# One block of a diffusion transformer on one core: an adaLN part moved in front of the MLP's normalization, VectorE's order there fixed, and the last rows of the first up products taken in two halves

## The chip, the core and the metric

The kernel runs on one core of one Trainium2 chip. What is measured is the time of one execution on the device in microseconds (us). A core has TensorE for products (PE in the profile, with its weight loads as PEld), VectorE (DVE), ScalarE (ACT), GpSimd (POOL), and SyncE (SP), whose queue issues nearly all loads here. All engines run side by side and wait for one another through semaphores. TensorE writes into eight PSUM banks.

## What is computed

One layer works on 256 latent tokens and 256 context tokens of width 2048, all in float32. Cut to what the change touches:

```python
sh_a, sc_a, g_a, sh_m, sc_m, g_m = split(silu(c) @ w_ada + b_ada)      # adaLN: 2048 x 12288
...                                                                     # attention and pooling mixer
x  = x + g_a * (concat(attn, pool) @ w_out)                             # 2048 x 2048
hm = rms_norm(x, norm_mlp_w) * (1 + sc_m) + sh_m
x  = x + g_m * (square(relu(hm @ w_up)) @ w_down)                       # 2048 x 8192 and back
return rms_norm(x, final_norm_w)
```

## The kernel before

**Products.** Each float32 weight block (512 rows by 512 columns, 1 MB) comes into a `raw` buffer, of which there are five, and is split into a high and a low part of a shorter format: ScalarE makes `hi` (line 97), VectorE `lo` (line 98), for 256 rows at a time, which is called a half. There are six `hi` and six `lo` buffers. The activations are split in the same way, and `mm3` makes each product of three: high by high, low by high, high by low (lines 288 to 290).

**The stream of loads.** `WeightStream` holds one list of all blocks in the order in which they are used. `next` issues loads up to five blocks ahead of the block that is handed out and splits up to six halves ahead. A load can start only when its `raw` buffer is free: the buffer of a weight block is free after both splits, that of an adaLN block after the engine that works on it has read it.

**adaLN parts.** The modulation of the MLP (`m0` to `m7`, 256 of its columns of scale and of shift each) and the attention gate (`g0` to `g3`) are computed in the gaps of later stages, in four blocks of 1 MB each, as `ADA_LATE` and the `LATE_...` numbers say. Parts marked "pe" are 32 small products per part (line 305, moving 128x512) and one copy `ada_e` (line 311); parts marked "dve" are sixteen VectorE instructions `ada_v` (lines 325 and 327) per part. `finish` then turns the row into columns with eight small products (`ps_adac`, line 335) and adds it into `am` and `sm` (lines 340 to 344). The finish of a part is called at the beginning of the step after its fourth.

**Around the change.** The output projection has four column groups (`out_group`), each of four weight blocks; beside them run `m2` to `m4` on VectorE. After a group VectorE multiplies by the gate and adds (lines 853 and 854), ScalarE sums squares (line 855), and TensorE transposes the new `x` into `x2T` (line 834). After the last group follows a chain: the sum of squares, its inverse root on VectorE (lines 862 to 866), a product that spreads it over partitions (`ps_r`, line 868), the copy `rb` (line 870), and then `modulate_m`, which makes four rows of `hm` of 128 channels each: `x2T` times `am` and `rb` (line 882), ScalarE's high part (line 884) and VectorE's low part (line 885). `first_up_groups` then works on three column groups of the up projection together, four rows after four rows (`kg`), with 48 products of 128x256 per block. `m5` runs on TensorE before its first products, `m6` and `m7` on VectorE beside them; the last rows (12 to 15) need `m6` and `m7`. Then come `down_group` and `up_group` in turn up to the end.

**What sets the order.** The program is traced in the order of the code; a scheduler then orders each engine's instructions by a timeline that it simulates, and keeps that order at run time: each engine takes its list in sequence. `tc.issue_after(ins)` forces what a block issues on the engine of `ins` behind `ins`. Some of the lines in question:

```python
LATE_OUT = (0, 1, 1, 1) * 4
LATE_NORM = 4
LATE_UP = (1,) * 8 + (0,) * 4
```

Of the kernel before, what the change touches and what calls it, by code (L numbers as in the profile page):

```python
# [15 lines left out]
P = 128  # L16
D = 2048
KC = 16
# [20 lines left out]
LATE_OUT = (0, 1, 1, 1) * 4  # L39
LATE_NORM = 4  # L40
LATE_UP = (1,) * 8 + (0,) * 4
# [17 lines left out]
class WeightStream:  # L59
# [7 lines left out]
    def __init__(self, nc, pool):  # L67
        self.nc, self.pool = nc, pool
        self.items, self.raw, self.split = [], {}, {}
        self.halves, self.n_load, self.n_half, self.n_used, self.pos = [], 0, 0, 0, 0  # L70
        self.hold, self.last = True, ()
# [16 lines left out]
    def split_to(self, n):  # L88
        nc = self.nc
        while self.n_half < min(n, len(self.halves)) and not self.hold:  # L90
# [8 lines left out]
            self.last = (up.ins, low.ins)  # L99
            self.split[i, h] = (hi, lo)  # L100
# [24 lines left out]
def kernel(  # L125
# [117 lines left out]

    for i in range(12):
        add_up(i % 3, i // 3)
        for _ in range(LATE_UP[i] + (LATE_NORM if i == 0 else 0)):
            add_in(("late",))
# [266 lines left out]
    def late_steps():  # L514
        for what, j, engine in ADA_LATE:
            ada, weights, spread = (ada_pe, sel, selb) if engine == "pe" else (ada_dve, ones[:, 0:2], ones)

            def finish(e, what=what, j=j, weights=weights, spread=spread):
                if what == "m":
                    k = slice(2 * j, 2 * j + 2)  # L520
                    ps = ada_cols(e, weights)
                    ada_scale(am[:, k], ps[:, 0:2], bcol[:, 64 + 2 * j : 66 + 2 * j], cols[:, 48 + 2 * j : 50 + 2 * j])
                    ada_shift(sm[:, k], ps[:, 2:4], bcol[:, 48 + 2 * j : 50 + 2 * j])
# [7 lines left out]
            yield from steps[:4]  # L531
            late_finish.append(steps[4])

    late_finish = []
    late_iter = late_steps()

    def run_late(n):

        for _ in range(n):
            f = next(late_iter, None)  # L540
            while late_finish:
                late_finish.pop()()
            if f:
                f()
# [292 lines left out]
    def out_group(dg):  # L837
# [11 lines left out]
        ds_ = slice(512 * dg, 512 * dg + 512)  # L849
        for i in range(2):  # L850
            t = wop.tile([P, 512], F32, tag="t", name="t", bufs=3)
            xs = x2[:, i, ds_]
            nc.vector.tensor_tensor(t, pss[i], gate["a"][:, ds_], ALU.mult)
            nc.vector.tensor_tensor(xs, xs, t, ALU.add)
            nc.scalar.activation(t, xs, AF.Square, accum_out=ss2[:, i, dg : dg + 1])

    for dg in range(4):
        out_group(dg)
    transpose_group(3)

# [16 lines left out]
    def modulate_m(kg):  # L877

        for j in range(4):
            k = 4 * kg + j  # L880
            v = x2T[kg][:, j, :]
            nc.vector.scalar_tensor_tensor(v, v, am[:, k, 0:1], rb, ALU.mult, ALU.mult)
            hi, lo, both = parts(k)
            nc.scalar.activation(hi, v, AF.Identity, bias=sm[:, k, 0:1])  # L884
            nc.vector.scalar_tensor_tensor(lo, v, sm[:, k, 0:1], hi.bitcast(F32), ALU.add, ALU.subtract)
            hm.append((hi, lo, both))
# [35 lines left out]
    def first_up_groups():  # L922
# [7 lines left out]
        modulate_m(0)  # L930
        for kg in range(4):
            for f in range(3):
                w = S.next("w")
                if kg == f == 0:
                    with tc.issue_after(rb_ready.ins):
                        run_late(LATE_NORM)
                for m in range(4):
                    for j in range(4):
                        k = 4 * kg + j
                        mm3(sums[f][m], w(j, slice(P * m, P * m + P)), hm[k], k == 0 and m % 2 == 0, k == KC - 1)  # L940
                with tc.issue_after(rb_ready.ins):
                    run_late(LATE_UP[3 * kg + f])
                    if kg == 2 and f == 1:
                        run_late(1)
                if kg < 3 and f == 1:
                    modulate_m(kg + 1)
                if kg == 3:
                    acts.append(activation(sums[f]))
# [153 lines left out]
```

## Time and profile before

| | us |
|---|---|
| median of 3 runs | 1146.16 |
| lowest and highest of them | 1143.71, 1147.84 |
| the profiled execution, whole | 1147.05 |
| span of its trace | 1145.3 |
| TensorE busy in it | 1104.6 (96%) |
| VectorE busy | 779.2 (68%) |
| ScalarE busy | 523.6 (46%) |
| GpSimd busy | 37.0 (3%) |

The trace is of one execution, with times counted from the beginning of its span. A matmul's row shows its duration from entry to result; matmuls overlap, so the distance from one start to the next tells the pace. A share of busy time is an average over stages with different limits, so it does not tell what a stage is worth.

### The profile page before, as it was taken

Reading aid. Unit: us, or ns where it says so; the run is one execution under the profiler, and the core shown is the slowest. Engines: PE = TensorE matmul, PEld = TensorE weight load, DVE = VectorE, ACT = ScalarE, POOL = GpSimd, SP = SyncE. Lnnn points to the kernel's source line nnn. Section 1 sums busy time; section 2 is a strip of 40 time slices with the busy share of each in tenths; the row PEclk is TensorE's granted clock in tenths of the full one; section 3 lists DMA queues with packets and bytes.
Section 4 is the critical chain, followed back from the end, with each engine's and each line's share of the span. In section 5 each row is a group of like instructions: output and inputs, shape, how many; then the busy total and the mean of one; then the engine's idle time right before and its main releaser. Section 6 shows DMA issues by size and latency. Waiting matters only on the chain.

```text
span 1145.3 us, 16131 instructions
## 1 busy us (share of the span) xinstructions
PE 1104.6 (96%) x6364; PEld 909.3 (79%) x6364; DVE 779.2 (68%) x1222; ACT 523.6 (46%) x796; POOL 37.0 (3%) x53
## 2 busy tenths in 40 slices
PE   4999999999999989999999999999999999999996
PEld 2767778856588869888888888888888888888885
DVE  4655567875588988696774874884664565587576
ACT  4633233499734343365343443433444443443452
POOL 1000001610000000000000000000000000000000
PEclk9999999999999989899999999999999999999998
DMA  9999898687799989977775776775566556566532
GB/s 343 359 341 336 288 325 264 210 292 259 267 369 314 325 306 332 336 246 259 262 265 184 257 269 195 253 267 192 184 192 202 194 184 185 191 192 204 184 110 75
DMA packets 174013, 286.66 MB, mean 250 GB/s; under 512 B 5608, under 2 KB 72352, under 8 KB 172784
## 3 DMA queue, kind: packets, MB, share of 16 engines
q1 hardware_dynamic: 172800, 279.55, 72.9%
q0 software_dynamic: 848, 5.55, 1.3%
q8 instruction: 50, 0.82, 0.3%
q10 hardware_dynamic: 288, 0.52, 0.1%
q14 instruction: 27, 0.22, 0.1%
HBM read 283.50 MB, written 2.10 MB: 249 GB/s over the span
## 4 chain that ended last, share of the span: by engine, by line
PE 88%; DVE 4%; ACT 3%; DMA 3%; issue 1%; SPq 0%; ACTq 0%; DVEq 0%
PE ps_up L919 25%; PE ps_d L288 10%; PE ps_d L289 10%; PE ps_d L290 10%; PE ps_ada L305 4%; PE ps_w L288 3%; PE ps_w L290 3%; PE ps_w L289 3%; PE ps_qu L288 2%; PE ps_qu L290 2%; PE ps_qu L289 2%; PE ps_up L288 1%; DVE lo L98 1%; PE ps_o L763 1%; PE ps_up L289 1%; PE ps_up L290 1%
## 5 line engine op out<-in xcount | busy, mean ns | idle before, releaser
L98 DVE TENSOR_TENSOR lo<-raw,hi 128x1024 fp32r<-128x1024 f32 x330 | 397.7, 1226 | 211.8 <-ACT hi L97 201.0
L97 ACT CAST hi<-raw 128x1024 fp32r<-128x1024 f32 x330 | 338.1, 1050 | 409.1 <-PE ps_up L919 151.7
L919 PE MATMUL ps_up<-mx,hi 128*128 128x512 f32 x832 | 200.1, 393 | 0.0
L288 PE MATMUL ps_d<-hi,ahi 128*128 128x512 f32 (+1 forms) x520 | 200.0, 386 | 0.0
L289 PE MATMUL ps_d<-lo,ahi 128*128 128x512 f32 (+1 forms) x520 | 200.0, 386 | 0.0
L290 PE MATMUL ps_d<-hi,alo 128*128 128x512 f32 (+1 forms) x520 | 198.7, 386 | 0.0
L919 PEld LDWEIGHTS ps_up<-mx,hi 128*128 128x128 f32 x832 | 153.4, 188 | 31.8 <-issue 1.9
L290 PEld LDWEIGHTS ps_d<-hi,alo 128*128 128x128 f32 x520 | 97.7, 188 | 19.8
L288 PEld LDWEIGHTS ps_d<-hi,ahi 128*128 128x128 f32 x520 | 97.7, 188 | 19.5
L289 PEld LDWEIGHTS ps_d<-lo,ahi 128*128 128x128 f32 x520 | 97.7, 188 | 19.3
L919 PEld LDWEIGHTS ps_up<-mx,lo 128*128 128x128 f32 x832 | 106.7, 191 | 4.0
L327 DVE SCALAR_TENSOR_TENSOR ada_v<-raw,c_sil,ada_v 128x512 f32<-128x512 f32 x135 | 100.9, 748 | 12.7 <-DMA raw<-in_w_ada_dram 11.1
L919 PE MATMUL ps_up<-mx,lo 128*128 128x256 f32 x832 | 107.9, 283 | 0.0
L288 PE MATMUL ps_qu<-hhi,hi 128*128 128x256 f32 x240 | 69.3, 290 | 1.4 <-ACT hi L97 1.4
L305 PE MATMUL ps_ada<-raw,c_sil 128*32 128x512 f32 x480 | 68.3, 628 | 2.2 <-DMA raw<-in_w_ada_dram 1.9
L290 PE MATMUL ps_qu<-hhi,lo 128*128 128x256 f32 x240 | 67.0, 282 | 0.3 <-DVE lo L98 0.3
L289 PE MATMUL ps_qu<-hlo,hi 128*128 128x256 f32 x240 | 66.9, 280 | 0.0
L288 PEld LDWEIGHTS ps_qu<-hhi,hi 128*128 128x128 f32 x240 | 45.1, 188 | 16.6 <-issue 8.4
L288 PE MATMUL ps_up<-mx,hi 128*128 128x256 f32 x192 | 54.7, 293 | 1.8 <-ACT mx L884 1.5
L289 PE MATMUL ps_up<-mx,hi 128*128 128x256 f32 x192 | 54.3, 287 | 0.0
L290 PE MATMUL ps_up<-mx,lo 128*128 128x256 f32 x192 | 53.1, 287 | 0.4 <-DVE lo L98 0.4
L288 PE MATMUL ps_w<-hi,mx 128*128 128x512 f32 x128 | 50.4, 395 | 0.0
(202 smaller groups left out, 1336.4 us busy)
## 6 DMA issues: line engine op xcount, KB each, us to landing
raw<-in_w_ada_dram SPq DMA_DIRECT2D x128, 512.0 KB, 7.3
raw<-in_w_mlp_up_dram SPq DMA_DIRECT2D x64, 1024.0 KB, 5.5
raw<-in_w_mlp_down_dram SPq DMA_DIRECT2D x64, 1024.0 KB, 5.1
raw<-in_w_ada_dram SPq DMA_DIRECT2D x32, 1024.0 KB, 6.8
raw<-in_w_in_dram SPq DMA_DIRECT2D x19, 1024.0 KB, 7.6
raw<-in_w_out_dram SPq DMA_DIRECT2D x16, 1024.0 KB, 7.5
xnat<-in_x_dram SPq DMA_DIRECT2D x2, 1024.0 KB, 6.0
xnat<-in_ctx_dram SPq DMA_DIRECT2D x2, 1024.0 KB, 11.7
```

Source lines behind the costliest of these rows:

```text
L97: up = nc.scalar.copy(hi, raw)
L98: low = nc.vector.tensor_tensor(lo, raw, hi.bitcast(F32), ALU.subtract)
L288: nc.tensor.matmul(ps, a[0], b[0], start=first, stop=False, skip_group_check=True)
L289: nc.tensor.matmul(ps, a[0], b[1], start=False, stop=False, skip_group_check=True)
L290: nc.tensor.matmul(ps, a[1], b[0], start=False, stop=last, skip_group_check=True)
L305: nc.tensor.matmul(ps[32 * j : 32 * j + 32, :], c_sil[:, 4 * kg + j, :], raw[:, j, :], start=(kg == 0), stop=(kg == 3), tile_position=(0, ...
L327: nc.vector.scalar_tensor_tensor(box["e"], raw[:, j, :], sc, box["e"], ALU.mult, ALU.add)
L763: nc.tensor.matmul(ps[64 * i : 64 * i + 64, 0:T], va[k // 2][:, k % 2, 64 * g : 64 * g + 64], pT[:, k, i, :], start=(k == 0), stop=(k == 3 ...
L919: nc.tensor.matmul(ps, wk, h, start=part == k == 0, stop=part == 1 and k == KC - 1, skip_group_check=True)
```

## The change

No weight block, product or VectorE operation is added or taken away; their order and places change.

- `LATE_OUT` shifts the twelve steps of `m2` to `m4`: one stands after the very first block of the output projection, and none after its last.
- The four blocks of `m5` come before the first up block in the list of loads. Their products are traced right behind the last output product (`behind_output`), ahead of VectorE's multiplication and addition and of the last transpositions. The small column products of `m4` stand behind them, those of `m5` behind the transpositions; what VectorE does with both (`rest`) is put off until after the first up block.
- The first up block (`up00` below) is no longer split ahead of time. Its first half is split behind the last addition of the output stage, its second behind the four VectorE instructions of line 882 for rows 0 to 3. Splits of later blocks come behind the low parts of rows 0 to 3.
- `modulate_m` takes a list of rows and makes all products with `am` and `rb` and the high parts first, then the low parts.
- The products with `up00` go in three passes: high by high over all rows and columns, low weights by high rows, high weights by low rows.
- Rows 12 to 15 are taken as 12 and 13 for all three column groups, then 14 and 15 for all three. Rows 14 and 15 are modulated behind `m7`'s finish. The three blocks of the last rows are all held at once, which takes all six half buffers; splits of the first down blocks are released as those halves are used up. The three `activation` calls come within the second pass.

```diff
-LATE_OUT = (0, 1, 1, 1) * 4
+LATE_OUT = (1, 1, 1, 1) + (0, 1, 1, 1) * 2 + (0, 1, 1, 0)
 LATE_NORM = 4
-LATE_UP = (1,) * 8 + (0,) * 4
+LATE_UP = (0,) + (1,) * 8 + (0,) * 3
...
+    for _ in range(LATE_NORM):
+        add_in(("late",))
     for i in range(12):
         add_up(i % 3, i // 3)
-        for _ in range(LATE_UP[i] + (LATE_NORM if i == 0 else 0)):
+        for _ in range(LATE_UP[i]):
             add_in(("late",))
...
+                    if put_off is None:
+                        rest()
+                    else:
+                        put_off.append(rest)
...
-    for dg in range(4):
+        return add.ins
+
+    for dg in range(3):
         out_group(dg)
+
+    def behind_output():
+
+        nonlocal put_off
+        before = late_finish[:]
+        late_finish.clear()
+        S.hold, put_off = True, []
+        run_late(LATE_NORM)
+        for f in before:
+            f()
+
+
+    added = out_group(3, behind_output)
+    S.hold = False
+    with tc.issue_after(added):
+        S.split_to(S.n_half + 1)
+    S.hold = True
     transpose_group(3)
+    finish_late()
+    late_rest, put_off = put_off, None
...
+    def modulate_m(ks, between=None):
+
+        new = [parts(k) for k in ks]
+        hm.extend(new)
+        for part in range(2):
+            for k, (hi, lo, _) in zip(ks, new):
+                v = x2T[k // 4][:, k % 4, :]
+                if part == 0:
+                    low = nc.vector.scalar_tensor_tensor(v, v, am[:, k, 0:1], rb, ALU.mult, ALU.mult)
+                    up = nc.scalar.activation(hi, v, AF.Identity, bias=sm[:, k, 0:1])
+                else:
+                    low = nc.vector.scalar_tensor_tensor(lo, v, sm[:, k, 0:1], hi.bitcast(F32), ALU.add, ALU.subtract)
+            if between and part == 0:
+                with tc.issue_after(low.ins):
+                    between()
+        return low.ins, up.ins
...
+        behind, up = modulate_m(range(4), second_half)
+        with tc.issue_after(behind), tc.issue_after(up):
+            w = S.next("w")
+
+            for a, h in ((0, 0), (1, 0), (0, 1)):
+                for k in range(4):
+                    for m in range(4):
+                        nc.tensor.matmul(sums[0][m], w(k, slice(P * m, P * m + P))[a], hm[k][h],
+                                         start=a == h == k == 0 and m % 2 == 0, stop=False, skip_group_check=True)
+            w = S.next("w")
+            behind = S.low[S.pos - 1, 1]
+            with tc.issue_after(behind):
+                for rest in late_rest:
+                    rest()
+                products(1, w, range(4))
+                run_late(LATE_UP[1])
+                modulate_m(range(4, 8))
+            products(2, S.next("w"), range(4))
+            run_late(LATE_UP[2])
+        for kg in (1, 2):
             for f in range(3):
...
+                products(f, S.next("w"), range(4 * kg, 4 * kg + 4))
+                run_late(LATE_UP[3 * kg + f])
+                if f == 1:
+                    modulate_m((8, 9, 10, 11) if kg == 1 else (12, 13))
+
+        used = S.n_used + N_HALF
+        ws = [S.next("w")]
+        finish_late()
+        modulate_m((14, 15))
+        S.hold = True
+        ws += [S.next("w") for _ in range(2)]
+        S.hold = False
+        for k, free in ((12, (1, 1, 1)), (14, (3, 5, 6))):
+            for f in range(3):
+                products(f, ws[f], (k, k + 1))
+                S.split_to(used + free[f])
+                if k == 14:
                     acts.append(activation(sums[f]))
         return acts
```

## Rows read from the trace of the kernel before

**Rows 1.** The page: busy time, share of the span and instructions per engine.

```profile
PE 1104.6 (96%) x6364; PEld 909.3 (79%) x6364; DVE 779.2 (68%) x1222; ACT 523.6 (46%) x796; POOL 37.0 (3%) x53
```

**Rows 2.** Stretches: busy PE, PEld, DVE, ACT, POOL; granted clock, DMA share, GB/s.

```profile
330.00:402.00 72.00, 72.00 (x340) 60.03 (x339) 62.22 (x81) 30.09 (x42) 0.00 (x0) 1.00 0.97 326
402.00:409.00 7.00, 3.01 (x20) 2.46 (x18) 5.09 (x24) 2.00 (x5) 0.55 (x1) 0.92 0.89 327
409.00:415.40 6.40, 6.40 (x33) 1.36 (x32) 6.40 (x20) 3.14 (x8) 0.00 (x0) 0.55 0.52 162
409.00:479.00 70.00, 67.15 (x529) 61.42 (x529) 60.19 (x97) 29.05 (x39) 0.00 (x0) 0.94 0.94 322
475.00:483.00 8.00, 6.05 (x31) 5.99 (x32) 5.16 (x12) 0.91 (x2) 0.00 (x0) 0.58 1.04 385
493.00:1134.00 641.00, 641.00 (x3229) 546.30 (x3229) 428.35 (x557) 279.18 (x371) 0.53 (x1) 1.00 0.63 208
```

**Rows 3.** Timeline of the first gap: start, duration, engine, line, tiles, idle before.

```profile
401.87 0.60 PE L834 MATMUL tp_x<-ident,x 128*128 128x128 f32 x4
...
404.33 0.16 DVE L862 TENSOR_REDUCE ssum<-ss 128x2 f32<-128x8 f32 x1 [0.85 <-ACT t L855]
...
408.31 3.26 DVE L882 SCALAR_TENSOR_TENSOR x2T<-x2T,am,rb 128x256 f32<-128x256 f32 x8
408.83 3.31 ACT L884 ACTIVATE mx<-x2T,sm 128x256 fp32r<-128x256 f32 x8 [4.02 <-DVE x2T L882]
...
409.00 6.49 PE L305 MATMUL ps_ada<-raw,c_sil 128*32 128x512 f32 x32
...
415.41 0.50 PE L288 MATMUL ps_up<-mx,hi 128*128 128x256 f32 x2
```

**Rows 4.** The chain that ended last: the same products where the clock is full.

```profile
242.11 3.57 PE ps_ada L305 x32
...
421.42 0.79 PE ps_adac L335 x8
```

**Rows 5.** Loads: splits that waited for one, the first gate product, issues on SP.

```profile
322.05 2.00 ACT L97 CAST hi<-raw 128x1024 fp32r<-128x1024 f32 x2 [6.07 <-DMA raw<-in_w_out_dram]
...
331.62 0.68 DVE L853 TENSOR_TENSOR t<-ps_w,ga 128x512 f32<-128x512 f32 x1
...
396.20 0.92 SPq L84 DMA_DIRECT2D raw<-in_w_ada_dram  x2
...
399.35 0.92 SPq L84 DMA_DIRECT2D raw<-in_w_ada_dram  x2
...
410.99 0.37 SPq L84 DMA_DIRECT2D raw<-in_w_mlp_up_dram  x1
```

**Rows 6.** Issue to landing (us, last number) of the loads issued at 396.20 and 399.35.

```profile
raw<-in_w_ada_dram SPq DMA_DIRECT2D x2, 512.0 KB, 7.3
...
raw<-in_w_ada_dram SPq DMA_DIRECT2D x2, 512.0 KB, 7.1
```

**Rows 7.** Timeline of VectorE: its longest wait in the first up products.

```profile
462.15 1.23 DVE L98 TENSOR_TENSOR lo<-raw,hi 128x1024 fp32r<-128x1024 f32 x1 [2.76 <-ACT hi L97]
```

**Rows 8.** Timeline of TensorE around the second gap.

```profile
475.44 1.13 PE L335 MATMUL ps_adac<-ones,ada_v 128*128 128x2 f32 x8 [0.67 <-DVE ada_v L327]
478.08 1.22 PE L288 MATMUL ps_up<-mx,hi 128*128 128x256 f32 x4 [1.51 <-ACT mx L884]
...
480.17 0.41 PE L289 MATMUL ps_up<-mx,hi 128*128 128x256 f32 x1
480.38 0.41 PE L290 MATMUL ps_up<-mx,lo 128*128 128x256 f32 x1
...
483.23 0.28 PE L288 MATMUL ps_up<-mx,hi 128*128 128x256 f32 x1
483.35 0.28 PE L289 MATMUL ps_up<-mx,hi 128*128 128x256 f32 x1
```

**Rows 9.** The first down products by tile: duration min/median/max, first and last start.

```profile
L288 PE MATMUL ps_d<-hi,ahi x520: 278/389/396, 493.3 to 1134.6; 128*128 128x512 f32 x168, 128*128 128x256 f32 x6
```

More of the change, by code (lines that the diff above doesn't have):

```diff
@@ L70, in __init__ @@
         self.halves, self.n_load, self.n_half, self.n_used, self.pos = [], 0, 0, 0, 0
-        self.hold, self.last = True, ()
+        self.hold, self.last, self.low = True, (), {}
     def add(self, kind, *loads, halves=2):
@@ L99, in split_to @@
             self.last = (up.ins, low.ins)
+            self.low[i, h] = low.ins
             self.split[i, h] = (hi, lo)
@@ L530, in late_steps, with last, finish_late @@
             steps = ada(finish)
-            yield from steps[:4]
-            late_finish.append(steps[4])
-    late_finish = []
+            yield from steps[:3]
+            def last(steps=steps):
+                steps[3]()
+                late_finish.append(steps[4])
+            yield last
+    late_finish, put_off = [], None
     late_iter = late_steps()
+    def finish_late():
+        while late_finish:
+            late_finish.pop(0)()
     def run_late(n):
@@ L835, in transpose_group, with out_group @@
             nc.scalar.copy(x2T[dg][:, :, P * i : P * i + P], tp.rearrange("p (j t) -> p j t", j=4))
-    def out_group(dg):
+    def out_group(dg, then=None):
         pss = [bank("ps_w0"), bank("ps_w1")]
@@ L849, in out_group @@
         ds_ = slice(512 * dg, 512 * dg + 512)
+        if then:
+            then()
         for i in range(2):
@@ L853, in out_group @@
             nc.vector.tensor_tensor(t, pss[i], gate["a"][:, ds_], ALU.mult)
-            nc.vector.tensor_tensor(xs, xs, t, ALU.add)
+            add = nc.vector.tensor_tensor(xs, xs, t, ALU.add)
             nc.scalar.activation(t, xs, AF.Square, accum_out=ss2[:, i, dg : dg + 1])
-    for dg in range(4):
+        return add.ins
+    for dg in range(3):
         out_group(dg)
+    def behind_output():
[11 more added lines that the diff above has]
+    S.hold = True
     transpose_group(3)
+    finish_late()
+    late_rest, put_off = put_off, None
     ssum = wop.tile([P, 2], F32, name="ssum")
@@ L875 @@
     hm = []
[L877 to L886, printed above, removed]
+    def modulate_m(ks, between=None):
[13 more added lines that the diff above has]
+        return low.ins, up.ins
     def activation(pss):
@@ L929, in first_up_groups, with products @@
         acts = []
-        modulate_m(0)
-        for kg in range(4):
-            for f in range(3):
[L933 to L947, printed above, removed]
+        def products(f, w, ks, ms=range(4)):
+            for m in ms:
+                for k in ks:
+                    mm3(sums[f][m], w(k % 4, slice(P * m, P * m + P)), hm[k], k == 0 and m % 2 == 0, k == KC - 1)
@@ new lines, in second_half @@
+        def second_half():
+            S.hold = False
+            S.split_to(S.n_half + 1)
+        behind, up = modulate_m(range(4), second_half)
[16 more added lines that the diff above has]
+            run_late(LATE_UP[2])
@@ new lines, in first_up_groups @@
+        for kg in (1, 2):
+            for f in range(3):
+                products(f, S.next("w"), range(4 * kg, 4 * kg + 4))
[4 more added lines that the diff above has]
+        ws = [S.next("w")]
+        finish_late()
+        modulate_m((14, 15))
+        S.hold = True
+        ws += [S.next("w") for _ in range(2)]
+        S.hold = False
+        for k, free in ((12, (1, 1, 1)), (14, (3, 5, 6))):
[3 more added lines that the diff above has]
+                if k == 14:
```

7 lines of the change are left out of this document (3 added, 4 removed).

## The prediction

> **What bounds the kernel now.** I read the page first: TensorE is busy 96% of the span [rows 1], so only its idle and its slow time can be won. Then I cut the span into stretches [rows 2]. From 330 to 402 TensorE is busy throughout at the full granted clock, and again from 493 to 1134 (641.00 of 641.00 us). What lies between holds two gaps. In the first, from 402 to 415.4, TensorE works 3 of 7 us and then 6.4 us at a mean clock of 0.55; in the second, from 475 to 483, it works 6 of 8 us at 0.58. The chance of the change is there and nowhere else: from 401.87, where the first transpositions follow the last output product [rows 3], to 493.3, where the down products begin [rows 9], 91.4 us. The products that must be done in that time, at the full pace: 12 blocks of 48 products, 0.12 us from start to start [rows 8], 69.1 us; `m5`, 3.57 us; columns of four parts, 0.79 us each [rows 4], 3.2 us; transpositions 1.2 us (two groups of four at 0.60 [rows 3]). That is 77.1 us without the small `ps_r`, so at most some 14 us can be won, 1.2% of the whole.
>
> The timeline of the first gap says who is late in it [rows 3]. VectorE's chain goes from the sum of squares at 404.33 to the first product with `rb` at 408.31. TensorE has nothing to do beside it but transpositions, and its clock falls. Only at 409.00 come the 32 products of `m5`, at half clock in 6.49 us, and the up products wait behind them until 415.41. In the second gap TensorE waits 0.67 us for VectorE's `m7`, computes its columns, waits 1.51 us for the rows made of it, and then runs at 0.21 us a product instead of 0.12 up to about 483.1 [rows 8].
>
> **The change, part by part.** Times are those of the profiled execution, 1147.05 us with a span of 1145.3; it lies 0.9 above the median of the three runs, 1146.16.
>
> *Steps of `m2` to `m4` one place earlier: 0.* In the first column group every output block now has a load of 1 MB in front of it. The first block of the second group landed at 322.05 and is needed at about 331.6, when the gate multiplies the first group [rows 5]; its two splits take until about 325.5. One more MB costs about 3.2 us at the 326 GB/s of this stretch [rows 2], so some 3 us of the margin stay, and TensorE's full row covers the shift. Without that cover it would cost up to 3 us; below nothing it can hardly go, since TensorE has no idle time there.
>
> *`m5` and the columns between the last output product and the MLP.* From 401.87 the 32 products end at 405.4, beside VectorE's chain. The columns of `m4` and `m5` (0.79 each), the transpositions and `ps_r` also fall under it. Their data: the last block of `m5` was issued at 396.20 and landed 7.3 us after its issue [rows 5, 6], at about 404.0; it moves one MB earlier in the list, to about 401. The products need it at 404.6, so I count no wait; with the old landing the wait is nil too.
>
> *VectorE's order.* The first half of `up00` now stands between the last addition (ended at about 403.5) and the sum of squares. Through `up00` the list holds as many MB as it did through the last block of `m5`, so I let it land at 404.0. ScalarE's half takes 1.0 (two in 2.00 [rows 5]), VectorE's 1.23 [rows 7]: the sum starts at 406.3, not 404.33, 2.0 later. If the weights are there in time, the lower bound is 0.4 (403.5 plus 1.23). The upper bound is `up00` landing like the old fifth block, issued at 399.35 and landed 7.1 after its second issue, at 407.0 [rows 5, 6]: 5.0 later. The middle value is nearest to the row of equal MB. VectorE waits with everything behind that half in hand, the whole chain and with it TensorE. The trace shows VectorE idle for 2.76 us at one half whose high part was late [rows 7]. [...]
>
> With 2.0, the first product with `rb` starts at 410.3. The first up product needs one such instruction (0.48) and one high part (0.5), so it starts at 411.3 instead of 415.41. High by high goes row by row, and VectorE makes a row every 0.41 us (8 in 3.26 [rows 3]) where TensorE takes four products, 0.48; the low weights' second half (1.2) and the low rows (four times 0.41) follow in time for passes of 1.92 us each. No wait there.
>
> *The clock.* Between 405.4 and 411.3 TensorE has some 3.5 us of small work. Before, it fell to half after such a stretch, before 409, and rose again near the end of `m5`. I count one fall: in the second gap some 24 products at 0.21 instead of 0.12 lost 2.2 us [rows 8]. Bounds: 0, and 2.9 (6.49 against 3.57 [rows 3, 4]). TensorE's own list then ends at 411.3 + 2.2 + 69.1 + 1.6 (columns of `m6` and `m7`) = 484.2.
>
> *VectorE as the next bound.* From 409 to 479, when it has made the last rows (TensorE takes the first of them at 478.08 [rows 8]), it is busy 60.2 of 70 us [rows 2]. Its work does not shrink: with 0.7 before 409 and the second half of `up00`, 1.2, it is 62.1 us from the first product with `rb`. Started at 410.3 it ends at 472.4 without idle time, and at 482.2 with the 9.8 us of before. Much of that idle time waits for loads. These stop when all five buffers are held: the first up load is issued only at 410.99, after the first products of `m5` [rows 5]; with those products at 402 it is issued about 8 us earlier. I keep 4 us of idle: 476.4. Behind it come 0.5 for the high and low part and the last 72 products (rows 14 and 15), 8.6: 485.5. That is later than TensorE's own 484.2, so VectorE ends the stage; the bounds are 484.2 and 491.3. Rows 12 and 13 come first and cover the finish of `m7`, which before stood bare.
>
> *Activations within the second pass.* From the end of the first group's sums, 5.8 before the end, to the second half of the first down group, 5.4 after it, VectorE has four low halves (4.9) and sixteen instructions of 128x256 (6.6 at 0.41), 11.5 us in 11.2. I add 0.8; bounds 0 and 2.8, the longest wait of before [rows 7]. Stage end: 486.3, against 493.3. **Gain 7.0 us.** Behind it TensorE has no idle time to swallow it [rows 2], so it lasts to the end: 1147.05 − 7.0 = 1140.05, and at the level of the median 1139.2; I say 1139.
>
> **The rivals.** *Both gaps close.* The half comes in time (0.4), the clock stays, VectorE idles 2 us. First product 409.7, TensorE's list 480.4, VectorE 408.7 + 62.1 + 2 + 9.1 = 481.9: gain 11.4, 1134.8. For it: TensorE is given work where it had none. Against: the small products have two columns each, and the clock fell beside such work in the second gap.
>
> *The half of `up00` takes the gap over.* It lands at 407.0, VectorE's start moves to 413.3; with 6 us of idle 413.3 + 62.1 + 6 + 9.1 + 0.8 = 491.3: gain 2.0, 1144.2. For it: loads stand at 0.97 of the DMA engines before 402, and five blocks lie between. Against: the equal number of MB.
>
> *The change does not do what it says.* The finish of `m7` is traced ahead of the products of rows 12 and 13. If the scheduler puts its columns amid the first pass on TensorE, TensorE waits for `m7` as before [rows 8]. With columns at 475.3 and half of the first pass behind them, 36 and 72 products, 13.0, and the clock's 2.2, the end is 490.5: gain 2.8, 1143.4. For it: the columns stood so in the trace of before. Against: in a simulated timeline that is right, the ready products go first.
>
> *Slower.* All six half buffers are held by the last rows, so down weights can be split only from 5.8 us before the end, beside three activations. It decides from the point at which VectorE brings rows 14 and 15 no earlier than it would with all its old idle time (stage end 491.3): then the first down block waits 2.8 for its low half and 2.8 for the second activation, and the clock falls once more (2.2): 499.1, 5.8 later than before, 1152. Against it: VectorE has 8 us of earlier loads.
>
> **How the numbers follow.** Forecast 0.43, both gaps close 0.20, the half takes over 0.14, not what it says 0.17, slower 0.06. A measurement of this kernel tells about 0.3% from no change, 3.4 us, so faster means under 1142.7. The forecast and the first rival lie under it, and I give a quarter of the second rival and a third of the third: 0.73 faster, 0.21 the same, 0.06 slower. The range reaches from the first rival's 1134 to 1144.7, above the second and third; it leaves out the slower case, and some of the bounds on either side.
>
> **What would show it.** In the profile after: `ps_ada` of `m5` in about 3.6 us right behind the last output product; the first up product near 411; the sum of squares near 406 with VectorE waiting in front of it for a high part; the granted clock at half for some us around 412; no wait of TensorE for `ada_v` after 465; the first down product near 486. I am wrong if TensorE waits in the output stage, if VectorE idles more than 6 us up to its last rows, if the columns of `m7` still hold TensorE, or if the down groups wait for halves.

## The result, and the profile after

The change makes the kernel slower: 1154.11 us median of 7 runs (1152.56 to 1157.12) against 1147.53 for the kernel before on the same chip (7 runs, 1143.71 to 1151.12), ratio 1.0064 with a 95% interval of 1.0049 to 1.0078. The forecast was 1139, its range 1134 to 1144.7. The profiled execution has a span of 1153.8 us, 8.5 more than before.

Three cuts show where they come from: the first instruction behind the last output product, the first up product, the first down product (starts on TensorE's timeline).

| | output stage ends | first up product | first down product | first gap | first up to first down |
|---|---|---|---|---|---|
| before | 401.87 | 415.41 | 493.30 | 13.5 | 77.9 |
| forecast | 401.87 | 411.3 | 486.3 | 9.4 | 75.0 |
| after | 407.27 | 415.73 | 502.03 | 8.5 | 86.3 |

The output stage ends 5.4 us later, the first gap is 5.1 shorter, the stretch behind it 8.4 longer: +8.7. Behind the first down product both kernels take the same time, 652.0 and 651.8 us.

The page of after: busy time, share and instructions per engine. It is nearly the row of before [rows 1] (TensorE 1.7 us more) and tells nothing of the loss.

```profile
PE 1106.3 (96%) x6364; PEld 910.2 (79%) x6364; DVE 779.8 (68%) x1222; ACT 523.6 (45%) x796; POOL 35.7 (3%) x53
```

Stretches of after (busy PE, PEld, DVE, ACT, POOL; granted clock, DMA share, GB/s): two at the start of the output stage, two of the first gap, the first up products up to the end of the first pass over the last rows, the second gap.

```profile
308.00:312.00 4.00, 3.04 (x7) 1.91 (x8) 0.95 (x2) 2.46 (x5) 0.00 (x0) 0.53 1.07 362
312.00:316.00 4.00, 4.00 (x13) 3.16 (x12) 2.75 (x3) 0.92 (x1) 0.00 (x0) 0.62 0.86 301
402.00:409.00 7.00, 7.00 (x40) 4.64 (x42) 2.97 (x5) 2.44 (x4) 0.55 (x1) 1.00 0.52 184
409.00:415.40 6.40, 5.15 (x46) 3.30 (x38) 4.69 (x23) 2.79 (x7) 0.00 (x0) 1.00 0.90 305
415.73:482.06 66.33, 63.90 (x512) 61.87 (x512) 57.76 (x88) 29.19 (x37) 0.00 (x0) 1.00 0.94 318
482.00:487.00 5.00, 0.11 (x2) 0.08 (x1) 4.77 (x6) 1.16 (x2) 0.00 (x0) 0.87 1.05 392
487.00:496.00 9.00, 6.56 (x30) 6.47 (x31) 6.53 (x14) 0.91 (x2) 0.00 (x0) 0.50 0.84 294
```

The first gap went as it should: the clock is 1.00 there, where it was 0.55 before [rows 2]. But TensorE's clock now falls near 308, where the output stage begins (0.53 from 308 to 312, 0.62 from 312 to 316), and TensorE stands still from 482 to 487 (busy for 0.11 of 5.00 us). The first place on the timelines of ScalarE and TensorE (start, duration, engine, line, tiles; in brackets the idle time before and what ended it):

```profile
305.18 1.99 ACT L97 CAST hi<-raw 128x1024 fp32r<-128x1024 f32 x2 [2.78 <-DMA raw<-in_w_out_dram]
307.34 1.08 ACT L772 COPY pT<-tp_p 128x512 f32<-128x512 f32 x2
308.96 1.11 PE L781 MATMUL ps_o<-pT,va 128*64 128x256 f32 x2 [3.66 <-ACT pT L772]
```

In ScalarE's list the high part of the second output block stands ahead of the last copies `pT` of the attention. The first step of `m2` now puts a load of 1 MB ahead of that block; it comes 2.78 us late for ScalarE, the copies wait behind it, TensorE waits 3.66 us for them, and its clock falls (0.53 from 308 to 312). The same two in the trace of before, where the block is 0.42 us late and TensorE waits 1.06:

```profile
301.49 1.99 ACT L97 CAST hi<-raw 128x1024 fp32r<-128x1024 f32 x2 [0.42 <-DMA raw<-in_w_out_dram]
306.48 0.65 PE L763 MATMUL ps_o<-pT,va 128*64 128x256 f32 x2 [1.06 <-ACT pT L754]
```

The second place on VectorE's and TensorE's timelines:

```profile
478.14 2.34 DVE L98 TENSOR_TENSOR lo<-raw,hi 128x1024 fp32r<-128x1024 f32 x2
480.41 0.74 DVE L330 SCALAR_TENSOR_TENSOR ada_v<-raw,c_sil,ada_v 128x512 f32<-128x512 f32 x1
481.20 2.36 DVE L98 TENSOR_TENSOR lo<-raw,hi 128x1024 fp32r<-128x1024 f32 x2
483.48 0.74 DVE L330 SCALAR_TENSOR_TENSOR ada_v<-raw,c_sil,ada_v 128x512 f32<-128x512 f32 x1
484.14 1.22 DVE L98 TENSOR_TENSOR lo<-raw,hi 128x1024 fp32r<-128x1024 f32 x1
485.27 1.53 DVE L330 SCALAR_TENSOR_TENSOR ada_v<-raw,c_sil,ada_v 128x512 f32<-128x512 f32 x2
486.95 1.84 PE L338 MATMUL ps_adac<-ones,ada_v 128*128 128x2 f32 x8 [4.89 <-DVE ada_v L330]
491.23 1.65 PE L291 MATMUL ps_up<-mx,hi 128*128 128x256 f32 x6 [2.44 <-ACT mx L926]
```

The 24 halves of the up blocks are split by 480.4; the three at 481.20 and 484.14 belong to down blocks, and `m7`'s last instructions stand behind them. TensorE ended its first pass at 482.06 and waits 4.89 us for `m7`, where it waited 0.67 before [rows 8]. Its columns then take 1.84 us, 2.44 us pass until the rows 14 and 15, and the second pass begins at the clock of the columns (0.50 from 487 to 496).

### The profile page after: what moved, and what is told of

It reads as the page before. It is cut to its first block, busy times and chain, and to the rows that moved or that the text cites. A ratio compares the mean times of both kernels' runs of the same rounds, so it can differ in the third digit from the quotient of the medians.

```text
span 1153.8 us, 16135 instructions
## 1 busy us (share of the span) xinstructions
PE 1106.3 (96%) x6364; PEld 910.2 (79%) x6364; DVE 779.8 (68%) x1222; ACT 523.6 (45%) x796; POOL 35.7 (3%) x53
## 4 chain that ended last, share of the span: by engine, by line
PE 83%; DMA 7%; DVE 5%; ACT 4%; issue 1%; SPq 1%; ACTq 0%; DVEq 0%
PE ps_up L965 25%; PE ps_d L292 10%; PE ps_d L293 10%; PE ps_d L291 10%; PE ps_ada L308 4%; DMA raw<-in_w_mlp_up_dram 4%; PE ps_w L291 3%; PE ps_w L292 3%; PE ps_w L293 3%; PE ps_qu L291 2%; PE ps_qu L293 2%; PE ps_qu L292 2%; DVE lo L98 2%; PE ps_o L781 1%; PE ps_adac L338 1%; ACT hi L97 1%
## 5 line engine op out<-in xcount | busy, mean ns | idle before, releaser
L965 PE MATMUL ps_up<-mx,lo 128*128 128x256 f32 x832 | 107.9, 283 | 0.0
L291 PE MATMUL ps_up<-mx,hi 128*128 128x256 f32 x176 | 49.9, 293 | 2.5 <-ACT mx L926 2.4
L293 PE MATMUL ps_up<-mx,lo 128*128 128x256 f32 x176 | 49.2, 291 | 2.4 <-DVE lo L98 2.0
L292 PE MATMUL ps_w<-lo,mx 128*128 128x512 f32 x128 | 50.6, 398 | 0.0
## 6 DMA issues: line engine op xcount, KB each, us to landing
xnat<-in_ctx_dram SPq DMA_DIRECT2D x2, 1024.0 KB, 11.8
```

What stands on the lines that cost most here:

```text
L291: nc.tensor.matmul(ps, a[0], b[0], start=first, stop=False, skip_group_check=True)
L292: nc.tensor.matmul(ps, a[0], b[1], start=False, stop=False, skip_group_check=True)
L293: nc.tensor.matmul(ps, a[1], b[0], start=False, stop=last, skip_group_check=True)
L965: nc.tensor.matmul(ps, wk, h, start=part == k == 0, stop=part == 1 and k == KC - 1, skip_group_check=True)
```

## The experiments

Twelve kernels in all; ratios are to the kernel before, measured beside each of them on the same chip (its median lay between 1146.72 and 1147.53), with 95% intervals. The cuts of their profiled executions are those of the table above:

| | median | ratio | output ends | first gap | first up to first down |
|---|---|---|---|---|---|
| after | 1154.11 | 1.0064 | 407.27 | 8.5 | 86.3 |
| e4_before_out | 1152.16 | 1.0041 | 405.00 | 13.5 | 78.1 |
| e1_out_start | 1158.22 | 1.0082 | 406.01 | 17.1 | 87.2 |
| e2_up_steps | 1155.59 | 1.0057 | 407.41 | 8.5 | 86.1 |
| e3_both | 1154.82 | 1.0063 | 401.92 | 11.7 | 85.4 |
| e5_down_behind | 1151.31 | 1.0041 | 409.08 | 8.5 | 83.3 |
| e6_half_behind | 1149.95 | 1.0036 | 400.99 | 8.8 | 85.8 |
| e7_all | 1149.23 | 1.0015 | 404.58 | 8.8 | 86.7 |
| e8_before_halves | 1145.55 | 0.9985 | 404.59 | 13.5 | 73.9 |
| e9_m5_halves | 1146.18 | 0.9995 | 403.77 | 7.5 | 82.4 |
| e10_m5_alone | 1152.94 | 1.0058 | 401.43 | 7.5 | 90.4 |
| e11_m6_pe | 1146.97 | 1.0007 | 408.32 | 8.5 | 76.9 |
| e12_all_m6_pe | 1144.19 | 0.9989 | 401.40 | 8.8 | 80.1 |

The end of the output stage differs by some us between executions of the same order of steps (400.99 to 406.01 with that of before, at least up to the last column group, 405.00 to 409.08 with that of after; the means, 402.95 and 407.42, are 4.5 apart), so I compare the last two columns from trace to trace, and totals by the medians. Each kernel has one trace, and those of e1, e5 and e7 are of their slowest execution (e5 3.1 us, e7 5.0 above its median), so a difference of a few us between two stretches is not certain by itself.

**The order of loads at the start of the output stage.** Theory A: the shifted steps cost the 5.4 us. On the kernel before:

```diff
-LATE_OUT = (0, 1, 1, 1) * 4
+LATE_OUT = (1, 1, 1, 1) + (0, 1, 1, 1) * 2 + (0, 1, 1, 0)
```

> The kernel before with nothing but the changed steps in the output stage. Theory A: TensorE waits some 3.7 us for the attention's copies at about 305 to 309, the clock falls after it, 5.3 us slower, ratio 1.0046. Rival (the start of the output stage suffers from the reordering of m5 and its loads, not from this): no change, ratio 1.000.

Measured 1.0041 (1.0026 to 1.0056), some 4.7 us, and the same picture on ScalarE and TensorE:

```profile
304.38 1.99 ACT L97 CAST hi<-raw 128x1024 fp32r<-128x1024 f32 x2 [3.09 <-DMA raw<-in_w_out_dram]
306.55 2.05 ACT L754 COPY pT<-tp_p 128x512 f32<-128x512 f32 x4
308.16 1.11 PE L763 MATMUL ps_o<-pT,va 128*64 128x256 f32 x2 [3.97 <-ACT pT L754]
```

A holds, by itself, in the kernel before. The other way round, in the kernel after:

```diff
-LATE_OUT = (1, 1, 1, 1) + (0, 1, 1, 1) * 2 + (0, 1, 1, 0)
+LATE_OUT = (0, 1, 1, 1) * 3 + (1, 1, 1, 0)
```

> The changed kernel with the loads at the start of the output stage as before (no adaLN step after the first block; the step is given back in the last column group, after its first block). Theory A (the second block's weights come one load later, ScalarE's list has their high part ahead of the last attention copies, TensorE waits and its clock falls): the output stage ends 5.3 us earlier than in the changed kernel, near 401.9; about 1149, a ratio to before of 1.001. Rival (what comes after is set by loads and VectorE in absolute time): the 5.3 us are given back before the first down product, which stays near 502; about 1154, ratio 1.006.

Measured 1.0082 (1.0046 to 1.0118), slower than after and with a wide spread (1150.69 to 1164.05; the profiled execution is the slowest of them). The wait at the start of the stage is gone (1.1 us for `pT`), but ScalarE and VectorE show a new one in the first gap:

```profile
416.07 1.99 ACT L97 CAST hi<-raw 128x1024 fp32r<-128x1024 f32 x2 [7.72 <-DMA raw<-in_w_mlp_up_dram]
417.14 1.23 DVE L98 TENSOR_TENSOR lo<-raw,hi 128x1024 fp32r<-128x1024 f32 x1 [7.34 <-ACT hi L97]
```

The half of `up00` that the change puts into VectorE's chain waits for its load, in the midst of the inverse root. The load was issued at 404.31, directly after VectorE's last instructions of `m4` (up to 404.28), and landed 11.8 us later. Later steps make later loads: here it is issued 1.70 us before the output stage ends, in after 7.29 (399.98). So the gain of the stage turned into a wait that the prediction had as a rival.

**The steps beside the up products.** Theory B: `m6` and `m7` are late because their steps and loads come one place later.

```diff
-LATE_UP = (0,) + (1,) * 8 + (0,) * 3
+LATE_UP = (1,) * 8 + (0,) * 4
...
+            run_late(LATE_UP[0])
             w = S.next("w")
             behind = S.low[S.pos - 1, 1]
```

> The changed kernel with the eight VectorE adaLN steps of m6 and m7 one place earlier again, in the list of loads and in the code (the first stands behind the first up block). Theory B (m7 comes late because its steps and loads stand one place, about 5.8 us, later): TensorE's wait for m7's columns goes from 9.3 us to under 4, the first down product to about 496; about 1148, ratio 1.001. Rival C (VectorE is full: it has the first block's splits to do as well, and order does not matter): m7's columns come less than 2 us earlier; 1152 to 1154, ratio 1.005.

Measured 1.0057 (1.0041 to 1.0074): B falls. `m6`'s columns came 3.0 us earlier than in after (452.95, not 455.95), but `m7`'s columns 0.7 us later, and TensorE's wait for `m7` was 4.86 us again. C's numbers are near, its reason (a full VectorE) is not what this trace shows in this place:

```profile
482.65 2.36 DVE L98 TENSOR_TENSOR lo<-raw,hi 128x1024 fp32r<-128x1024 f32 x2 [1.54 <-PE ps_up L292]
484.93 0.75 DVE L330 SCALAR_TENSOR_TENSOR ada_v<-raw,c_sil,ada_v 128x512 f32<-128x512 f32 x1
485.59 1.22 DVE L98 TENSOR_TENSOR lo<-raw,hi 128x1024 fp32r<-128x1024 f32 x1
486.73 0.75 DVE L330 SCALAR_TENSOR_TENSOR ada_v<-raw,c_sil,ada_v 128x512 f32<-128x512 f32 x1
```

The down halves wait until TensorE's first pass frees a half buffer, `m7`'s end stands behind them, and TensorE waits for `m7` behind its first pass: VectorE can be early as it will, the wait is about what lies between (2.36, 0.75, 1.22 and 0.75). With both edits:

> Both of these together. Theories A and B: the two losses add and what is left is the first gap's gain of 5 us less a rest of the second gap; about 1143, ratio 0.996. Rival C: about 1148, ratio 1.001.

Measured 1.0063 (1.0037 to 1.0089), near neither value. The output stage ended at 401.92, but the half of `up00` kept VectorE waiting, and TensorE waited 4.07 us for `m7`:

```profile
407.08 1.99 ACT L97 CAST hi<-raw 128x1024 fp32r<-128x1024 f32 x2 [2.82 <-DMA raw<-in_w_mlp_up_dram]
408.16 1.23 DVE L98 TENSOR_TENSOR lo<-raw,hi 128x1024 fp32r<-128x1024 f32 x1 [2.44 <-ACT hi L97]
484.93 1.12 PE L338 MATMUL ps_adac<-ones,ada_v 128*128 128x2 f32 x8 [4.07 <-DVE ada_v L330]
```

**The down halves, and the half of up00.** Two theories from these traces, each with its edit. D: the down halves hold `m7`; they come behind the rows 14 and 15 (in the kernel after):

```diff
-        modulate_m((14, 15))
+        rows, _ = modulate_m((14, 15))
...
-                S.split_to(used + free[f])
+                with tc.issue_after(rows):
+                    S.split_to(used + free[f])
```

> The kernel after, with one edge more: the splits of the down blocks that are released inside the two passes of the last rows come on VectorE behind the rows 14 and 15. In the trace of after three of them (1.22 us each) stand ahead of the last products of m7, and TensorE waits 4.89 us for m7. Theory D (these halves hold m7): m7 ends 3.7 us earlier, TensorE's wait falls from 4.9 to about 1.2, its clock stays up, the first down product comes near 498, and the median is about 1150.3, ratio 1.0025 to the kernel before. Rival (VectorE is full through the stage, so what is put behind comes back): the wait for m7 goes, but the activations and the first down products then wait for the halves, and the median stays at 1153.5 to 1155, ratio 1.0055 or more.

Measured 1.0041 (1.0025 to 1.0057), 2.8 us below after, where 3.8 were expected; the two intervals overlap, so the trace has to carry the reading. TensorE's wait for `m7` falls to 1.61, but 4.12 us pass until the rows:

```profile
485.22 1.02 PE L338 MATMUL ps_adac<-ones,ada_v 128*128 128x2 f32 x8 [1.61 <-DVE ada_v L330]
488.11 0.48 DVE L328 TENSOR_SCALAR ada_v<-raw,c_sil 128x512 f32<-128x512 f32 x1 [1.59 <-DMA raw<-in_w_ada_dram]
490.37 1.65 PE L291 MATMUL ps_up<-mx,hi 128*128 128x256 f32 x6 [4.12 <-ACT mx L926]
```

The next in VectorE's list, ahead of the rows, is the first instruction of the following adaLN part, and its block is 1.59 us late. D holds for its own size, and the next late load takes a part back. In e3_both, the half taken out of the chain:

```diff
-    S.hold = False
-    with tc.issue_after(added):
-        S.split_to(S.n_half + 1)
-    S.hold = True
-    transpose_group(3)
+    x2T_ready = transpose_group(3)
...
             S.hold = False
-            S.split_to(S.n_half + 1)
+            with tc.issue_after(x2T_ready):
+                S.split_to(S.n_half + 2)
```

> The kernel with both lists of steps as in before (run e3_both), with the first half of up00 no longer split behind the last addition: both halves come behind the four products with rb, on ScalarE behind the copies of the last transpositions. In e3_both VectorE waited 2.44 us for this half in the middle of the inverse root, beside 1.23 of work, and the first up product came at 413.6. If that half holds the chain: first up product near 410, 3.5 us earlier, and the median about 1151.3, ratio 1.0035. If the later loads or the end of the first pass set the time whatever the start, the first pass gets longer by as much, and the median stays near 1154.5, ratio 1.006.

Measured 1.0036 (1.0022 to 1.0050), as expected of a half that holds the chain: the first gap falls from 11.7 to 8.8 us, and the median by 4.9. Both edits together:

> Both edits of e5_down_behind and e6_half_behind on the kernel with both lists of steps as in before (e3_both). If the output stage (5.3 us), the half in the chain (3.5) and the down halves ahead of m7 (4) are what the change lost, and each is worth its size: the first up product near 410, TensorE's wait for m7 under 1 us, first down product near 491.5, the median about 1147, ratio 1.000 (0.998 to 1.002). If VectorE is full and only passes the loss on: 1152 or more, ratio 1.004.

Measured 1.0015 (1.0000 to 1.0029), 2.2 us above the expected 1147. TensorE no longer waits for `m7` (its columns come at 484.85 without a wait). But in this trace, of the slowest of its twelve executions, the stretch up to the down products is 86.7 us long: VectorE and TensorE wait for high parts whose loads are late (VectorE 10.3 us in all, 8.1 in after), and the clock is at 0.68 from 485 to 495.

**One part alone, on the kernel before.** The last rows in halves, with the released down halves behind the rows 14 and 15:

```diff
-                    if kg == 2 and f == 1:
-                        run_late(1)
-                if kg < 3 and f == 1:
-                    modulate_m(kg + 1)
-                if kg == 3:
-                    acts.append(activation(sums[f]))
+                if f == 1:
+                    modulate_m(kg + 1, range(4) if kg < 2 else (0, 1))
+        used = S.n_used + N_HALF
+        ws = [S.next("w")]
+        with tc.issue_after(rb_ready.ins):
+            run_late(1)
+        rows = modulate_m(3, (2, 3))
...
+        for ks, free in (((12, 13), (1, 1, 1)), ((14, 15), (3, 5, 6))):
...
+                with tc.issue_after(rows):
+                    S.split_to(used + free[f])
```

> The kernel before with one part of the change alone: rows 12 to 15 in two halves (12 and 13 for all three groups, then 14 and 15), the activations inside the second pass, the released down halves behind the rows 14 and 15 on VectorE. Output stage, first gap and steps of the adaLN parts are those of before. If the halves do what they were costed at once m7 is not held up: the second gap of before (0.7 of wait for m7, 1.5 for the rows, 2.2 of half clock) closes, first down product near 489 instead of 493.3, the median about 1142.8, ratio 0.9963. If the halves themselves cost what they give (VectorE's activations late, down products waiting for halves): 1147 to 1150, ratio 1.000 to 1.003.

Measured 0.9985 (0.9972 to 0.9997): faster, by less than half of the expected 4.4 us. In the trace the stretch is 4.0 us shorter, but the output stage of this execution ended 2.7 us later than in that of before. TensorE does not wait for `m7` at all, and its clock stays up through the first pass; the wait for the rows remains:

```profile
418.11:480.34 62.23, 62.23 (x523) 62.23 (x520) 51.73 (x72) 27.10 (x31) 0.00 (x0) 1.00 1.00 345
480.34 0.95 PE L335 MATMUL ps_adac<-ones,ada_v 128*128 128x2 f32 x8
483.12 0.98 PE L288 MATMUL ps_up<-mx,hi 128*128 128x256 f32 x6 [1.60 <-ACT mx L884]
```

Then `m5` behind the last output product, with `up00` loaded and split ahead of it, as before, on e8_before_halves and on the kernel before:

```diff
+    def behind_output():
+        nonlocal hold_finish, up00
+        S.hold = hold_finish = True
+        up00 = S.next("w")
+        run_late(LATE_NORM)
+        hold_finish = False
...
-                w = S.next("w")
                 if kg == f == 0:
-                    with tc.issue_after(rb_ready.ins):
-                        run_late(LATE_NORM)
+                    w, S.hold = up00, False
+                    with tc.issue_after(first[0]), tc.issue_after(first[1]):
+                        S.split_to(S.n_used + N_AHEAD)
```

> The kernel e8_before_halves with the 32 products of m5 traced behind the last output product, as in the change, but in the order of loads of before: up00 is loaded and split ahead of m5's blocks, so that no half stands in VectorE's chain; the splits of up10 come behind the rows 0 to 3. Expected if the first gap's gain reaches the end: first up product near 409.5 after an output stage that ends near 402 (7.6 us between, before 13.5), first down product 5.9 us earlier than in e8, the median about 1139.6, ratio 0.993. If the loads and VectorE set the first pass (four kernels with a shorter first gap had a first pass of 66 to 71 us where e8 had 62), the first pass gets longer by what the gap gives: median 1145 to 1147, ratio 0.998 to 1.000.

Measured 0.9995 (0.9982 to 1.0008). The first gap is 7.5 us as expected, 6 less than in e8, and more than that is lost behind it in the trace (the stretch is 8.5 longer), but not as I had put it: the clock takes most of it, a late load a smaller part. Stretches of e9 from its first up product, and TensorE's wait in them:

```profile
411.27:423.30 12.03, 9.72 (x51) 9.63 (x52) 10.64 (x27) 6.50 (x11) 0.00 (x0) 0.57 1.07 368
423.30:480.99 57.69, 57.54 (x479) 57.30 (x478) 47.21 (x63) 22.77 (x27) 0.00 (x0) 1.00 0.88 296
416.88 0.80 PE L288 MATMUL ps_up<-mx,hi 128*128 128x256 f32 x2 [2.31 <-ACT hi L97]
```

For 12 us the granted clock is 0.57: it falls at 412, while TensorE does sixteen column products; then TensorE waits 2.31 us for a late high part and runs on slowly, a product every 0.21 us until 422.4 and every 0.12 from there. An estimate from these times: 8.1 us of work at half the pace cost 4.0, beside the 2.31 of the load. In the kernel before the slow time fell on `m5` (0.55 [rows 2]); in e9, where `m5` comes ahead, it falls on the columns and the up products (0.57).

> The kernel before with m5's products behind the last output product alone (order of loads, steps and last rows as in before). Expected if the first gap's gain reaches the end: first up product 5.9 us earlier, median about 1141.5, ratio 0.995. If the loads and VectorE set the time of m7's end whatever the start of the up products: TensorE's wait for m7 grows from 0.7 to about 6 and the median stays at 1147, ratio 1.000.

Measured 1.0058 (1.0040 to 1.0077), worse than either value. The clock is at 0.61 from 408.9 to 414.9 and at 0.83 from there to 420.9 (in e9 0.57 and 0.58 in the twelve microseconds from the first up product). At the end of the stretch VectorE waits for blocks of the following adaLN part, and TensorE for VectorE:

```profile
477.42 1.02 PE L335 MATMUL ps_adac<-ones,ada_v 128*128 128x2 f32 x8 [2.25 <-DVE ada_v L327]
482.17 0.49 DVE L325 TENSOR_SCALAR ada_v<-raw,c_sil 128x512 f32<-128x512 f32 x1 [3.45 <-DMA raw<-in_w_ada_dram]
484.43 1.65 PE L288 MATMUL ps_up<-mx,hi 128*128 128x256 f32 x6 [5.98 <-ACT mx L893]
```

That instruction has nothing to do with rows 12 to 15, but it stands ahead of them in VectorE's list, and they wait with it: 3.45 us on VectorE, 5.98 on TensorE.

**VectorE's work.** The last question is whether loads or VectorE set the stretch. One word changed, in after and in e7_all:

```diff
-("m", 6, "dve")
+("m", 6, "pe")
```

> The kernel after with one word changed: m6 is computed by TensorE (32 products, 3.6 us at full clock) instead of VectorE (16 instructions, 0.48 + 15 x 0.746 = 11.7 us). Blocks loaded, their order and the last rows stay. If VectorE's work sets the end of the stage from the first up product to the first down product (86.3 us in after, where products and columns need some 71): m7 ends about 10 us earlier, TensorE's waits for m7 and for halves (9.3 us in after) mostly go, 3.6 us of products come in, stage about 79, the median about 1147, ratio 1.000. If the loads set it (20 MB between the output stage and the last up block, at the 300 to 340 GB/s of the trace): VectorE idles for its data instead, the wait for m7 stays and the products of m6 come on top: 1154 to 1158, ratio 1.006 or more.

Measured 1.0007 (0.9995 to 1.0019), 1146.97 where VectorE's theory had 1147. Stretches of e11, from the first up product to `m7`'s columns and on to the first down product:

```profile
416.78:475.48 58.70, 58.70 (x472) 53.84 (x473) 46.31 (x72) 26.50 (x35) 0.00 (x0) 1.00 1.05 366
475.48:493.65 18.17, 18.17 (x155) 18.17 (x153) 14.59 (x24) 9.23 (x15) 0.00 (x0) 1.00 0.78 262
```

TensorE is busy throughout at full clock, though it does 3.6 us more. The loads, the same blocks in the same order, now run at 366 GB/s and a share of 1.05; in after it was 318 and 0.94. So they were not late by themselves: they waited for buffers that VectorE read late. SyncE's issues in after show it: five of these loads come within 0.03 us of the end of one of VectorE's low halves (432.96, 439.24, 446.19, 452.94, 459.92), and the waits of its queue for low halves come to 27.0 us between 405 and 490. VectorE still waits for high parts in e11 (11.0 us, 8.1 in after), but with less in its list (busy for 46.3 of 58.7 us, in after for 57.8 of 66.3) TensorE no longer waits for it: its one wait from 416 to 495 is 1.6 us, at the first up product.

> The same word changed in e7_all (steps as in before, half of up00 out of the chain, down halves behind the last rows; there VectorE waited 10.3 us for high parts whose loads were late, and TensorE did not wait for m7). If VectorE's work holds back the loads, which wait for buffers that it reads: stage from 86.7 to about 79, the median about 1143, ratio 0.996. If the loads are late by themselves: 1149 to 1153, ratio 1.002 or more.

Measured 0.9989 (0.9977 to 1.0001), 1144.19, 1.2 us above the expected 1143 and the lowest median of all. The stretch is 80.1 us, not 79: at its start the clock is 0.65 for 10 us, and TensorE waits 2.3 us for the first block of `m6`.

## Why the prediction was wrong

**The output stage: costed 0, measured +5.4 (e4 alone: 4.7 by the ratio).** The step took the margin from the first block of the second column group [rows 5]. The block that becomes late is the second of the first group. I asked when a product needs it, and not what stands behind its high part on ScalarE: the last copies of the attention, which TensorE waits for. "TensorE's full row covers the shift" was wrong, since that row does not begin before these copies.

**The first gap: right.** 9.4 us forecast, 8.5 measured. `m5` took 3.64 us right behind the last output product, 3.57 was forecast. The half of `up00` cost its 1.22 without a wait (2.0 counted), and the one fall of the clock (2.2) did not come there (1.00 from 402 to 420). That is luck: behind the same gap it came in e2_up_steps (0.66 from 415 to 420, last section). The rows of after's first gap:

```profile
407.27 3.64 PE L308 MATMUL ps_ada<-raw,c_sil 128*32 128x512 f32 x32
407.29 2.00 ACT L97 CAST hi<-raw 128x1024 fp32r<-128x1024 f32 x2 [0.46 <-DMA raw<-in_w_mlp_up_dram]
408.71 1.22 DVE L98 TENSOR_TENSOR lo<-raw,hi 128x1024 fp32r<-128x1024 f32 x1
409.93 0.16 DVE L902 TENSOR_REDUCE ssum<-ss 128x2 f32<-128x8 f32 x1
414.19 0.42 DVE L910 COPY rb<-ps_r 128x256 f32<-128x256 f32 x1 [1.54 <-PE ps_r L908]
415.73 2.18 PE L992 MATMUL ps_up<-mx,hi 128*128 128x256 f32 x16 [1.58 <-ACT mx L926]
```

That the half did not wait goes with the shifted steps themselves. In all four traces that have them and the half in the chain (after, e2, e5, e11) the load of `up00` is issued 7.1 to 7.3 us before the output stage ends, whenever that is, and VectorE does not wait for it; in e3_both and e1, with the steps put back, it is issued 3.1 and 1.7 us before, and VectorE waits 2.44 and 7.34. So the order of steps that costs the output stage its 5 us also pays for this term, and the rival "the half takes the gap over" comes as soon as one takes that order back.

**The stretch behind it: 75.0 forecast, 86.3 measured.** This is the larger error, 11.3 us, and lies in the step "VectorE as the next bound". That VectorE's work would be the bound was right, as e11 shows; three terms of its sum were not. VectorE's stretch from the first product with `rb` to the last rows, in after and then in before:

```profile
414.65:492.40 77.75, 66.91 (x525) 64.82 (x526) 67.12 (x105) 31.77 (x41) 0.00 (x0) 0.96 0.96 328
408.31:478.90 70.59, 67.74 (x532) 62.00 (x533) 60.84 (x98) 29.22 (x39) 0.00 (x0) 0.94 0.93 319
```

It began at 414.65, not 410.3 (4.35, from the output stage less what the gap gave). It had 67.1 us of work, not 62.1: three down halves (3 × 1.22) and the first three instructions of the next adaLN part, which the scheduler's list has ahead of the rows 14 and 15. It was idle for 10.6, not 4. That is 4.35 + 5.0 + 6.6 = 16.0, and the rows came at 492.4 where 476.4 was forecast. The term of 4 us was an argument that earlier loads give less idle time; most of the idle time (8.1 us) is still waiting for high parts, and VectorE itself releases the buffers for those loads (the issue times under e11). I had taken the down halves for a danger behind the rows (the slower rival); they were one ahead of them.

**What of the rest.** The halves came as the text said: `m7`'s columns stood behind the first pass, so the third rival did not occur. In this part the clock did fall once, but behind `m7` (0.50 from 487 to 496). Activations and down products did not wait: from 493 on TensorE is busy without a break, as before. The slower rival named the right engine and a wrong place, and 0.06 was too little for it: its point of decision, old idle time in VectorE, was just what the traces of before showed. (A slip of addition: the shares given to "faster" and "the same" come to 0.72 and 0.22, not 0.73 and 0.21.)

**What stays open.** Why VectorE waited longer for high parts in e7_all than in after was not taken apart. With `m6` on TensorE these waits do not go (11.0 us in e11, 15.6 in e12); TensorE only no longer waits for VectorE behind them. That one word takes 11.7 us of work off VectorE and also has TensorE read four blocks in its place; which of the two counts was not separated. Nor was it asked why the output stage ends some us apart in executions with the same steps. Of e1's spread of 13 us one execution was seen. No kernel here is faster than before by 0.3%: e8 by 0.15%, its interval just under 1; e12 has 0.9989, its interval just over.

## What to carry to other kernels

Before work is moved into a gap of TensorE, add up the list of the engine that feeds the stage behind it, with everything that the scheduler may put ahead of the last needed instruction; if that list is the bound, take work off it (one word here, 7 us), since a shorter gap alone came back here as a wait or as a slow clock (0.57 for 12 us and a wait of 2.31 in e9, a wait of 5.98 in e10). The load that was moved up here made the block behind it 3.09 us late for ScalarE (e4; 0.42 in before), and its price was found at the engine that splits the late block, where TensorE waited 3.97 us for the copies behind that split (1.06 in before): see what stands behind such a split in its list. Where splits of the next stage wait for buffers that this stage frees, force them behind the last instruction that this stage waits for (e5: the wait for `m7` fell from 4.89 to 1.61 us).

## What the runs showed of the hardware

The clock fell behind one first gap and not behind another of the same kind. Stretches of after and then of e6, from `m5` to the first up product, and of e6 behind it:

```profile
407.27:415.73 8.46, 6.88 (x60) 3.85 (x59) 6.61 (x26) 4.84 (x9) 0.55 (x1) 1.00 0.72 248
400.99:409.79 8.80, 7.11 (x59) 3.82 (x59) 5.59 (x26) 4.73 (x9) 0.55 (x1) 1.00 1.03 367
409.79:416.00 6.21, 6.21 (x39) 6.21 (x40) 4.73 (x9) 1.61 (x4) 0.00 (x0) 0.73 1.08 372
```

TensorE is busy 81% of both gaps with the same products at full clock. In after it stays there (1.00 up to 420); in e6 it falls as the up products begin (0.73), though they come without a break (busy for 6.21 of 6.21 us). In e2_up_steps the gap is that of after to the hundredth, the same 60 products busy for 6.88 of 8.46 us at 1.00, and the clock falls behind it all the same: 0.66 from 415 to 420. So the list of products in the gap does not decide it, and what does, these rows don't tell; a fall of the clock can be forecast here only with both ends.

The share of the DMA engines that after shows in the first up products was not the most that these loads could get: the same blocks in the same order ran at 0.94 and 318 GB/s in after and at 1.05 and 366 in e11, where the one thing changed was `m6`, taken from VectorE's list.
